# The last column group of x2 turned by VectorE out of DRAM, the loads of two gates moved, one store moved

## The chip, the cores and the metric

The kernel runs on one core of a Trainium2 chip. The metric is device time in microseconds; the median of three runs before the change is 1065.82 us (1065.55 to 1066.18). Times inside the kernel are from one execution taken by the hardware profiler, counted from its first instruction. Engines are called by their names: PE or TensorE (products and transposes), PEld (TensorE's loading of weights), DVE or VectorE, ACT or ScalarE, POOL or GpSimd, SP or SyncE, which only issues DMAs here. ScalarE issues DMAs too; a `q` behind an engine's name in a view (SPq, ACTq) marks what its sequencer issued.

## The reference

One layer of a decoder trunk, 512 tokens (T) by 2048 features (D), in float32:

```
h = rms_norm(x, norm_g);  z = h @ w_in          # RWKV streams, gates, pool input
y_mix = concat([y_rwkv * silu(g_rwkv), y_pool * pool_scale * silu(g_pool)])
x2  = x + y_mix @ w_out
gate = sigmoid(x2 @ w_pg + b_pg)
x3  = x2 + gate * (p @ w_ple)
out = rms_norm(x3, final_g)
```

The change touches only what lies behind the recurrence: x2, the gate, x3 and the last norm.

## The kernel before

**Products in three parts.** Every operand of a large product is split into a high part (a copy rounded to a narrower float32 format) and a low part (the remainder); `mm3` adds high x high, high x low and low x high in PSUM. The copy is ScalarE's, the subtraction VectorE's: `wsplit` (L127 to L136) for a tile of weights, which also issues the load from DRAM on SP's queue, and `split` (L140 to L143) for activations. `wsplit` leaves its three instructions in `wmade`: the DMA, the copy, the subtraction. The pool `wp` has four buffers each for `raw`, `whi` and `wlo`, so copies run up to four steps ahead of TensorE, and loads up to four steps ahead of the copies.

**The two last projections.** `proj` makes one group of 512 output columns: 16 steps over the 128-row slices k of the contraction, in each step four row tiles of 128 tokens (`acc[tt]`), three products each. It runs four times for `w_out` (the products are called `acc_o` in the trace, k in the sequence `order`) and then four times for `w_pg` (`acc_g`, k from 0 to 15). The contraction of `w_pg` runs over the columns of x2, so x2 is needed transposed: `x2hi` and `x2lo`, 16 tiles of 128 columns by 512 tokens. Column group `ec` of `w_out` makes the tiles 4 ec to 4 ec + 3.

**How x2 is transposed.** When a group of `w_out` is done, VectorE adds x (L1123) and ScalarE's queue stores the tile to `x2d` in DRAM (L1124). For the first three groups `turner` does the rest beside the next group's products: at each step `proj` calls `side(i)`, which from step `RD0` = 5 on issues three reads a step on SP's queue (L1135), 16 in all, of 64 KB each. A read brings a 32-row strip of a tile in such a way that VectorE's transpose of 32x32 blocks (L1141, at the steps `TURNS` = 8, 9, 11, 12) then gives the transposed tile, which `split` takes apart. Blocks lie in `x2g`, turned tiles in `x2t`. The last group (ec = 3) has no next group of `w_out`; there `turn` (L1146 to L1152) transposes with TensorE against the identity, 16 times 128x128 into PSUM (`px`), inside the first group of `w_pg`: `proj` calls `aside` at step 2.

**The gates.** For each group and row tile of `w_pg`, `gate` adds `bB` (the bias, VectorE, L1195), takes the tanh (ScalarE, L1197), combines with `pler` (p @ w_ple, made before and kept in DRAM; L1203) and with `x2r` (x2, read back; L1204), squares, and multiplies by `gB`. Their loads are DMAs of ScalarE: `recall` (four `pler`, L1112), `vectors` (`bB` and `gB`, L1171 and L1173), `fetch` (one `x2r` per row tile, L1251).

**What sets the order.** A scheduler sorts each engine's instructions, by program order and by when its model holds them ready; each engine then runs its list in order. `tc.issue_after(i)` puts the instructions of its block that are on `i`'s engine behind `i` in that list. A DMA has to wait for its turn on the queue of the engine that issues it.

**The end.** After the last product the last row tile is scaled and stored in four pieces of 512 columns in the sequence 0, 1, 3, 2, by SP (L1247). Pieces 1 and 2 are scaled by ScalarE, the others by VectorE.

Of the kernel before, what the change touches and what calls it, by code (L numbers as in the profile page):

```python
# [9 lines left out]
F32 = mybir.dt.float32  # L10
# [5 lines left out]
P = 128  # L16
T = 512
D = 2048
KT = D // P
NT = T // P  # L20
# [14 lines left out]
def trunk_kernel(ctx: ExitStack, tc: tile.TileContext, x, p, norm_g, w_in, mu, w0, w_up, a0, a_up,  # L35
                 k_k, k_a, r_k, ln_w, ln_b, w_pool, pool_scale, w_out, w_ple, w_pg, b_pg, final_g, out):
    nc = tc.nc
    PSUM = bass.MemoryType.PSUM
    x, p, w_in, w_out, w_ple, w_pg = x[0], p[0, 0], w_in[0], w_out[0], w_ple[0], w_pg[0]
    out = out[0]  # L40
# [53 lines left out]
    for h in range(2):  # L94
        rows = slice(64 * h, 64 * h + 64)
# [44 lines left out]
    def split(hi, lo, src):  # L140
        c_ = nc.scalar.copy(hi, src)
        nc.vector.tensor_tensor(lo, src, hi.bitcast(F32), ALU.subtract)
        return c_  # L143
# [920 lines left out]
    def proj(w, hi_, lo_, ec, nm, ks=range(KT), tts=range(NT), keep=None, side=None, aside=None):  # L1064
        acc = {tt: acc_tile(f"acc_{nm}{ec}_{tt}") for tt in tts}
        for i, k in enumerate(ks):
            src = w[k * P:(k + 1) * P, ec * EC:(ec + 1) * EC].unsqueeze(1)
            if nm == "o" and ec == 0 and i + AHEAD < KT:
                load_y(ks[i + AHEAD])
            if (f"{nm}{ec}_{k}", 0) in ready:  # L1070
                wh, wl = ready.pop((f"{nm}{ec}_{k}", 0))
            elif nm == "o" and ec == 0 and i < 4:
                wh, wl = chunk(f"{nm}{ec}_{k}", 0)
            elif keep is None or LATE <= i < KT - KEEP:
                wh, wl = wsplit(src, 1, EC, f"{nm}{ec}_{k}")
            else:
                raw = wp.tile([P, 1, EC], F32, name=f"raw_{nm}{ec}_{k}", tag="raw")
                nc.sync.dma_start(out=raw, in_=src)
                if i < 2:
                    if i == 0:  # L1080
                        two = [pp.tile([P, 2, EC], F32R, name=f"{g}k", tag=g, bufs=1) for g in ("dh", "dl")]
                    wh, wl = (g[:, i:i + 1, :] for g in two)
                else:
                    own = i < KT - 4
                    wh, wl = ((kp_ if own else wp).tile([P, 1, EC], F32R, name=f"{g}k{k}",
                                                        tag=f"{g}k{k}" if own else g) for g in ("whi", "wlo"))
                split(wh, wl, raw)
                keep[k] = (wh, wl)
                if i >= LATE:
                    continue  # L1090
            if aside is not None and i == 2:
                with tc.issue_after(e_.ins):
                    hi = aside()
                with tc.issue_after(hi.ins):
                    recall(0, lp)
            if side is not None:
                side(i)
            for tt in tts if keep is None or i >= LATE else tts[:-1]:
                ts_ = slice(tt * P, (tt + 1) * P)
                first = i == (LATE if keep is not None and tt == NT - 1 else 0)  # L1100
                e_ = mm3(acc[tt], hi_[:, k, ts_], lo_[:, k, ts_], wh[:, 0, :], wl[:, 0, :], first, i == KT - 1)
        return acc
# [5 lines left out]
    def recall(ec, pool):  # L1108
        ples[ec] = []
        for tt in range(NT):  # L1110
            t_ = pool.tile([P, EC], F32, name=f"pler{ec}_{tt}", tag="ple", bufs=4)
            nc.scalar.dma_start(out=t_, in_=pled[tt * P:(tt + 1) * P, ec * EC:(ec + 1) * EC])  # L1112
            ples[ec].append(t_)

    for ec in range(D // EC):
        es = slice(ec * EC, (ec + 1) * EC)
        acc = proj(w_out, yhi, ylo, ec, "o", order, side=side)
        x2 = []
        for tt in range(NT):
            rows = slice(tt * P, (tt + 1) * P)  # L1120
            t_ = pp.tile([P, EC], F32, name=f"x2_{ec}_{tt}", tag=("u", "sw")[tt // 2])
            nc.scalar.dma_start(out=t_, in_=x[rows, es])
            nc.vector.tensor_tensor(t_, acc[tt], t_, ALU.add)  # L1123
            nc.scalar.dma_start(out=x2d[ec, :, rows, :].rearrange("c t e -> t c e"),  # L1124
                                in_=t_.rearrange("p (c e) -> p c e", e=P))
            x2.append(t_)

        def turner(blocks, turned, ec=ec):
            parts = [(c, q) for c in range(EC // P) for q in range(4)]

            def side(i):
                with tc.issue_after(wmade[0].ins), tc.issue_after(wmade[1].ins), tc.issue_after(wmade[2].ins):
                    if i >= RD0:
                        for c, q in parts[:RDN]:
                            nc.sync.dma_start(out=blocks[32 * q:32 * q + 32, c],  # L1135
                                              in_=x2d[ec, c].rearrange("(b k) (q i) -> q k b i", k=32, i=32)[q])
                        del parts[:RDN]
                    if i in TURNS:
                        c = TURNS.index(i)
                        t_ = turned(c)  # L1140
                        nc.vector.transpose(t_.rearrange("p (b k) -> p b k", k=32), blocks[:, c])  # L1141
                        split(x2hi[:, 4 * ec + c, :], x2lo[:, 4 * ec + c, :], t_)

            return side

        def turn(ec=ec, x2=x2):  # L1146
            for i in range(EC // P):
                pt = psM.tile([P, T], F32, name=f"px2_{ec}_{i}", tag="m")
                for tt in range(NT):
                    nc.tensor.transpose(pt[:, tt * P:(tt + 1) * P], x2[tt][:, i * P:(i + 1) * P], ident)  # L1150
                hi = split(x2hi[:, 4 * ec + i, :], x2lo[:, 4 * ec + i, :], pt)
            return hi  # L1152

        if ec < D // EC - 1:
            side = turner(ymp.tile([P, EC // P, T // 32, 32], F32, name=f"x2g{ec}", tag="x2g"),
                          lambda i: ymp.tile([P, T], F32, name="x2t", tag="x2t"))
# [4 lines left out]
    with tc.tile_pool(name="fp", bufs=2) as fp, tc.tile_pool(name="kp_", bufs=1) as kp_:  # L1161
        x3 = [fp.tile([P, D], F32, name=f"x3_{tt}", bufs=1) for tt in range(NT)]
        ssq = [fp.tile([P, D // EC + 1], F32, name=f"ssq{tt}", bufs=1) for tt in range(NT)]
        LAST = D // EC - 1
        WIDE, ENDS = 256, 6
        kept = {}

        def vectors(ec):
            es = slice(ec * EC, (ec + 1) * EC)
            bB = fp.tile([P, EC], F32, name=f"bB{ec}", tag="bB")  # L1170
            nc.scalar.dma_start(out=bB, in_=b_pg[0:1, es].to_broadcast([P, EC]))  # L1171
            gB = fp.tile([P, EC], F32, name=f"gB{ec}", tag="gB")
            nc.scalar.dma_start(out=gB, in_=final_g[es].unsqueeze(0).to_broadcast([P, EC]))  # L1173
            return bB, gB

        sq = [None]

        def behind(i, of):

# [52 lines left out]
        def scaled(tt, rs, gts, pcs):  # L1232
            rows = slice(tt * P, (tt + 1) * P)
            for pc_ in pcs:
                ps_ = slice(pc_ * EC, (pc_ + 1) * EC)
                if pc_ == LAST:
                    o_ = 0
                    for g_ in gts:
                        w_ = g_.shape[-1]
                        nc.vector.scalar_tensor_tensor(x3[tt][:, ps_.start + o_:ps_.start + o_ + w_], g_, rs,  # L1240
                                                       vec[1][:, o_:o_ + w_], ALU.mult, ALU.mult)
                        o_ += w_
                elif pc_ in ((1, 2) if tt == NT - 1 else (1,)):
                    nc.scalar.activation(x3[tt][:, ps_], x3[tt][:, ps_], AF.Copy, scale=rs)
                else:
                    nc.vector.tensor_scalar(x3[tt][:, ps_], x3[tt][:, ps_], rs, None, ALU.mult)
                nc.sync.dma_start(out=out[rows, ps_], in_=x3[tt][:, ps_])  # L1247

        def fetch(ec, tt):
            x2_ = fp.tile([P, EC], F32, name=f"x2r{ec}_{tt}", tag="x2r", bufs=4)  # L1250
            nc.scalar.dma_start(out=x2_.rearrange("p (c e) -> p c e", e=P),  # L1251
                                in_=x2d[ec, :, tt * P:(tt + 1) * P, :].rearrange("c t e -> t c e"))
            pre[tt] = (x2_, ple[tt])

        for ec in range(LAST):
            pre = {}
            vec = vectors(ec)
            acc = proj(w_pg, x2hi, x2lo, ec, "g", aside=turn if ec == 0 else None)
            ple = ples.pop(ec)
            recall(ec + 1, fp if ec % 2 == 0 else lp)  # L1260
            for tt in range(NT):
                fetch(ec, tt)
                gate(acc[tt], ec, tt, slice(ec * EC, (ec + 1) * EC), ec)
        ec = LAST
        ple = ples.pop(ec)
# [64 lines left out]
```

## Time and profile before

| what | us |
|---|---|
| median of three runs | 1065.82 (1065.55 to 1066.18) |
| the profiled execution | 1066.03 |
| its span, first to last instruction | 1064.3 |
| products of `w_out` start | 704.4 |
| products of `w_pg` start | 878.4 |
| last product starts | 1055.1 |

The span is that of the instructions; 1.7 us of the execution's own time lie around it. In the views a row of the timeline is: start, length, engine, line, operation, output<-inputs, shape, count, and in brackets the idle time of that engine before it with what ended it. A row "x12" stands for twelve instructions merged. The chain of waits is followed back from the last instruction, at each step to what released it; its pieces are start, length, engine and tile. Lengths of single products overlap, since TensorE takes the next one in before the last has left; the distance of their starts is the pace.

### The profile page before, as it was taken

To read this page: it belongs to the slowest core of one execution; us is meant where nothing else is said; L and a number is where in the kernel's file an instruction comes from. 1 tells how busy PE (TensorE), PEld (TensorE's weight loads), DVE (VectorE), ACT (ScalarE), POOL (GpSimd) and SP (SyncE) were. 2 spreads that over 40 slices of the span, in tenths; PEclk is the share of its full clock that TensorE was granted. 3 is DMA by queue.
4 is the path that set the end of the run, shared out by engine and by line. 5 is a ranking of instruction groups with operands and counts; after the bars stand their busy time and mean duration, and the time that the engine had idled before them with its cause. 6 is when DMAs were issued, how large, how long until landed. Compare 5 with 4: busy or idle time off the path is not lost.

```text
span 1064.3 us, 17220 instructions
## 1 busy us (share of the span) xinstructions
PE 1040.8 (98%) x5884; PEld 861.4 (81%) x5884; DVE 714.1 (67%) x1878; ACT 434.0 (41%) x893; POOL 75.6 (7%) x180
## 2 busy tenths in 40 slices
PE   5999999999999999999999999999999999999996
PEld 4888888888888888878888788888888888888885
DVE  6687878878788689797877968553444343535456
ACT  7633424434334344344442344543222232324336
POOL 2100011010110101201101102000000000000000
PEclk9999999999999999999999999999999999999998
DMA  7444453554555635545447364774846649355434
GB/s 239 108 119 122 124 127 78 156 147 105 163 121 137 157 87 151 144 114 150 117 114 186 84 160 132 240 244 142 208 149 176 173 137 277 125 182 173 155 99 158
DMA packets 292173, 159.08 MB, mean 149 GB/s; under 512 B 130305, under 2 KB 254826, under 8 KB 292086
## 3 DMA queue, kind: packets, MB, share of 16 engines
q1 hardware_dynamic: 264070, 129.41, 44.6%
q10 hardware_dynamic: 28016, 28.58, 8.7%
q8 instruction: 46, 0.75, 0.3%
q14 instruction: 41, 0.34, 0.1%
HBM read 130.63 MB, written 26.79 MB: 148 GB/s over the span
## 4 chain that ended last, share of the span: by engine, by line
PE 84%; DVE 3%; issue 1%; ACT 0%; DMA 0%; ACTq 0%; DVEq 0%
PE acc_o L161 16%; PE acc_g L161 16%; PE zb L161 14%; PE zg L161 7%; PE zv L161 6%; PE zr L161 6%; PE zk L161 6%; PE pple L161 2%; PE py L161 2%; PE pu L161 2%; PE pm L161 1%; PE ps L161 1%; PE pp L161 1%; PE pmv L161 1%; DVE sw L418 1%
## 5 line engine op out<-in xcount | busy, mean ns | idle before, releaser
L134 DVE TENSOR_TENSOR wlo_g<-raw_g,whi_g 128x512 fp32r<-128x512 f32 x84 | 57.3, 689 | 81.5 <-ACT whi_g L133 81.5
L161 PE MATMUL zb<-hhi,whi_b 128*128 128x512 f32 x256 | 105.2, 411 | 0.0
L161 PE MATMUL zb<-hhi,wlo_b 128*128 128x512 f32 x256 | 100.4, 392 | 0.0
L161 PE MATMUL zb<-hlo,whi_b 128*128 128x512 f32 x256 | 99.9, 390 | 0.0
L161 PE MATMUL acc_o<-whi_o,ylo 128*128 128x512 f32 x256 | 99.7, 390 | 0.0
L161 PE MATMUL acc_o<-wlo_o,yhi 128*128 128x512 f32 x256 | 99.7, 389 | 0.0
L134 DVE TENSOR_TENSOR wlo_o<-raw_o,whi_o 128x512 fp32r<-128x512 f32 x64 | 43.9, 690 | 79.3 <-ACT whi_o L133 79.2
L161 PE MATMUL acc_o<-whi_o,yhi 128*128 128x512 f32 x256 | 94.8, 389 | 0.0
L133 ACT CAST whi_g<-raw_g 128x512 fp32r<-128x512 f32 x84 | 51.9, 620 | 103.7 <-PE acc_g L161 57.4
L161 PE MATMUL acc_g<-whi_g,x2hi 128*128 128x512 f32 x208 | 81.3, 391 | 0.0
L161 PE MATMUL acc_g<-wlo_g,x2hi 128*128 128x512 f32 x208 | 81.1, 390 | 0.0
L161 PE MATMUL acc_g<-whi_g,x2lo 128*128 128x512 f32 x208 | 80.8, 390 | 0.0
L904 POOL TENSOR_SCALAR s0p<-sbd,pw 64x64 f32<-64x64 f32 x96 | 57.6, 600 | 324.4 <-DVE sbd L897 246.3
L133 ACT CAST whi_o<-raw_o 128x512 fp32r<-128x512 f32 x64 | 39.4, 621 | 94.2 <-PE acc_o L161 58.4
L133 ACT CAST whi_b<-raw_b 128x512 fp32r<-128x512 f32 x64 | 39.4, 620 | 51.7 <-PE zv L161 16.4
L134 DVE TENSOR_TENSOR wlo_b<-raw_b,whi_b 128x512 fp32r<-128x512 f32 x64 | 43.9, 688 | 21.8 <-ACT whi_b L133 20.8
L721 DVE TENSOR_TENSOR xw<-xw,tm 128x60 f32<-128x60 f32 (+24 forms) x248 | 52.3, 211 | 6.8
L161 PEld LDWEIGHTS zb<-hhi,wlo_b 128*128 128x128 f32 x256 | 48.0, 188 | 10.8
L878 ACT COPY uv<-pu 64x64 f32<-64x64 f32 x128 | 26.3, 205 | 73.4 <-PE pu L161 72.4
L161 PEld LDWEIGHTS acc_o<-whi_o,yhi 128*128 128x128 f32 x256 | 48.1, 188 | 10.0
L161 PEld LDWEIGHTS acc_o<-wlo_o,yhi 128*128 128x128 f32 x256 | 48.1, 188 | 10.0
L161 PEld LDWEIGHTS acc_o<-whi_o,ylo 128*128 128x128 f32 x256 | 48.1, 188 | 9.9
(293 smaller groups left out, 2516.9 us busy)
## 6 DMA issues: line engine op xcount, KB each, us to landing
raw_b<-in_w_in_dram SPq DMA_DIRECT2D x64, 256.0 KB
raw_o<-in_w_out_dram SPq DMA_DIRECT2D x64, 256.0 KB
raw_g<-in_w_pg_dram SPq DMA_DIRECT2D x64, 256.0 KB
raw_k<-in_w_in_dram SPq DMA_DIRECT2D x32, 256.0 KB
raw_r<-in_w_in_dram SPq DMA_DIRECT2D x32, 256.0 KB
raw_v<-in_w_in_dram SPq DMA_DIRECT2D x32, 256.0 KB
raw_g<-in_w_in_dram SPq DMA_DIRECT2D x32, 256.0 KB
bkd<-bk SPq DMA_DIRECT2D x8, 512.0 KB
```

The lines of the kernel that those rows point to most:

```text
L133: made.append(nc.scalar.copy(hi, raw))
L134: made.append(nc.vector.tensor_tensor(lo, raw, hi.bitcast(F32), ALU.subtract))
L161: i = nc.tensor.matmul(*a, **k)
L418: nc.vector.tensor_tensor(n_[:, w_:T], s_[:, w_:T], s_[:, 0:T - w_], ALU.add)
L721: nc.vector.tensor_tensor(xw[:, 0:n_, s + 1:32], xw[:, 0:n_, s + 1:32], tm[:, 0:n_, 0:w_], ALU.add)
L878: u_ = nc.scalar.copy(uv[pb:pb + 64, ch, hc], psu[hc, hc])
L904: nc.gpsimd.tensor_scalar(s0p[hc, :], nxt[hc, hc], pcn[hc], None, ALU.mult)
```

## The change

1. `turn` and its 16 transposes are removed. The last group gets a `turner` of its own, with `x3[0]` for the blocks and slices of `x3[1]` for the turned tiles (both are written only later, by the gates). `proj` of the first group of `w_pg` calls its `side`: reads from step 6 on, three a step, turns at the steps 9, 10, 11 and 13.
2. The first group's `recall` and `vectors`, which stood ahead of the group or at its third step, are issued at its step 12 behind ScalarE's copy of that step's weights (`begin`). The second group's `recall` and the `fetch` of each gate are put behind that copy too.
3. The last row tile's store of piece 2 is issued by ScalarE, not SP.

```diff
-            if aside is not None and i == 2:
-                with tc.issue_after(e_.ins):
-                    hi = aside()
-                with tc.issue_after(hi.ins):
-                    recall(0, lp)
+            if aside is not None and i == 12:
+                with tc.issue_after(wmade[1].ins):
+                    aside(wmade[1])
...
-        def turner(blocks, turned, ec=ec):
+        def turner(blocks, turned, ec=ec, rd0=RD0, rdn=RDN, turns=TURNS):
...
-        def turn(ec=ec, x2=x2):
-            for i in range(EC // P):
-                pt = psM.tile([P, T], F32, name=f"px2_{ec}_{i}", tag="m")
-                for tt in range(NT):
-                    nc.tensor.transpose(pt[:, tt * P:(tt + 1) * P], x2[tt][:, i * P:(i + 1) * P], ident)
-                hi = split(x2hi[:, 4 * ec + i, :], x2lo[:, 4 * ec + i, :], pt)
-            return hi
...
+        side = turner(x3[0].rearrange("p (c b k) -> p c b k", c=EC // P, k=32), lambda i: x3[1][:, i * T:(i + 1) * T],
+                      rd0=6, rdn=3, turns=(9, 10, 11, 13))
...
+        def begin(e_):
+            nonlocal vec
+            recall(0, lp)
+            vec = vectors(0)
+            begun_.append(e_)
...
-                nc.sync.dma_start(out=out[rows, ps_], in_=x3[tt][:, ps_])
+                (nc.scalar if tt == NT - 1 and pc_ == 2 else nc.sync).dma_start(out=out[rows, ps_], in_=x3[tt][:, ps_])
...
-            vec = vectors(ec)
-            acc = proj(w_pg, x2hi, x2lo, ec, "g", aside=turn if ec == 0 else None)
+            if ec:
+                vec = vectors(ec)
+            acc = proj(w_pg, x2hi, x2lo, ec, "g", side=side if ec == 0 else None, aside=begin if ec == 0 else None)
             ple = ples.pop(ec)
-            recall(ec + 1, fp if ec % 2 == 0 else lp)
+            with tc.issue_after(begun_[0].ins):
+                recall(ec + 1, fp if ec % 2 == 0 else lp)
             for tt in range(NT):
-                fetch(ec, tt)
+                with tc.issue_after(begun_[0].ins):
+                    fetch(ec, tt)
                 gate(acc[tt], ec, tt, slice(ec * EC, (ec + 1) * EC), ec)
```

More of the change, by code (lines that the diff above doesn't have):

```diff
@@ L1132, in side @@
                 with tc.issue_after(wmade[0].ins), tc.issue_after(wmade[1].ins), tc.issue_after(wmade[2].ins):
-                    if i >= RD0:
-                        for c, q in parts[:RDN]:
+                    if i >= rd0:
+                        for c, q in parts[:rdn]:
                             nc.sync.dma_start(out=blocks[32 * q:32 * q + 32, c],
                                               in_=x2d[ec, c].rearrange("(b k) (q i) -> q k b i", k=32, i=32)[q])
-                        del parts[:RDN]
-                    if i in TURNS:
-                        c = TURNS.index(i)
+                        del parts[:rdn]
+                    if i in turns:
+                        c = turns.index(i)
                         t_ = turned(c)
@@ L1176, in trunk_kernel @@
         sq = [None]
+        begun_ = []
+        def begin(e_):
[3 more added lines that the diff above has]
+            begun_.append(e_)
+        vec = None
         def behind(i, of):
```

## The prediction

> **What bounds the kernel now.** I read the page's busy shares and chain first, then the chain of waits over the place of the change, then who waits there, then the timeline of each queue that the change touches.
>
> ```profile
> PE 1040.8 (98%) x5884; PEld 861.4 (81%) x5884; DVE 714.1 (67%) x1878; ACT 434.0 (41%) x893; POOL 75.6 (7%) x180
> 704.52 174.08 PE acc_o L161 x768
> 878.60 5.44 PE acc_g L161 x24
> 884.04 1.31 PE px L1150 x12
> 885.35 1.16 PE acc_g L161 x5
> 886.51 0.44 PE px L1150 x4
> 886.95 73.11 PE acc_g L161 x322
> ```
>
> The first row is the page's, the others are pieces of the chain (start, length, what). TensorE is busy 98% of the span, and from 704.5 us the chain is TensorE alone: all of `w_out`, then `w_pg`. 768 products took 174.08 us, so a product starts every 0.2267 us and a step of `proj` (four row tiles, three products each) takes 2.72 us. The only pieces that are not products of the projections are the 16 transposes `px`. What matters here is therefore (a) what TensorE no longer does and (b) whether something new makes it wait.
>
> ```profile
> PEld acc_g L161 <- DVE gt L1195: 0.2, 1, 0.2
> 883.65 0.39 PE L161 MATMUL acc_g<-whi_g,x2lo 128*128 128x512 f32 x1
> 883.88 1.47 PE L1150 MATMUL px<-ident,x 128*128 128x128 f32 x12
> 885.11 0.48 PE L161 MATMUL acc_g<-whi_g,x2hi 128*128 128x512 f32 x1
> 885.43 0.39 PE L161 MATMUL acc_g<-wlo_g,x2hi 128*128 128x512 f32 x1
> 886.12 0.39 PE L161 MATMUL acc_g<-wlo_g,x2hi 128*128 128x512 f32 x1
> 886.35 0.60 PE L1150 MATMUL px<-ident,x 128*128 128x128 f32 x4
> 886.71 0.48 PE L161 MATMUL acc_g<-whi_g,x2lo 128*128 128x512 f32 x1
> 887.02 0.39 PE L161 MATMUL acc_g<-whi_g,x2hi 128*128 128x512 f32 x1
> ```
>
> The first row is the only wait of TensorE in the view of waits from 835 to 930 us: 0.2 us, at the first gates. The rest is its timeline around the transposes.
>
> **Part 1, the transposes go.** From product to product where 0.227 us is usual: 883.65 to 885.11 is 1.23 too long, 885.11 to 885.43 is 0.09, 886.12 to 886.71 is 0.36, 886.71 to 887.02 is 0.08. Together 1.8 us (the chain's `px` pieces alone give 1.31 + 0.44 = 1.75). No wait hides behind them, so this is all that can go: **-1.8 us**.
>
> **Part 2, the blocks from DRAM.** In their place come 16 reads of 64 KB on SP's queue, four transposes on VectorE, and the same four pairs of ScalarE copy and VectorE subtraction, now out of SBUF. The kernel does exactly this already for the first three column groups, beside `w_out`; the last of these stages starts at 704.52 + 3 x 43.52, near 835.0 us.
>
> ```profile
> 838.51 0.33 SPq L130 DMA_DIRECT2D raw_o<-in_w_out_dram  x1
> 840.97 6.75 SPq L1135 DMA_DIRECT2D x2g<-x2d  x9
> 847.82 0.43 SPq L130 DMA_DIRECT2D raw_o<-in_w_out_dram  x1
> 851.78 0.62 ACT L133 CAST whi_o<-raw_o 128x512 fp32r<-128x512 f32 x1 [5.17 <-DMA raw_o<-in_w_out_dram]
> 852.44 0.43 SPq L1135 DMA_DIRECT2D x2g<-x2d  x1
> L1141 DVE STREAM_TRANSPOSE x2t<-x2g x12: 702/704/706, 765.4 to 866.3; 128x512 f32<-128x512 f32 x12
> 869.07 0.68 DVE L142 TENSOR_TENSOR x2lo<-x2t,x2hi 128x512 fp32r<-128x512 f32 x1
> 887.02:924.91 37.89, 37.89 (x169) 31.36 (x168) 12.11 (x19) 10.33 (x17) 0.00 (x0) 1.00 0.64 208
> ```
>
> Here nine reads stood ahead of the weights of step 8 (of 0 to 15), whose copy began at 851.78; with copy and subtraction (0.62 + 0.69) they were there near 853.1. Step 8 runs at 835.0 + 8 x 2.72 = 856.7, so 3.6 us were left, and the chain row of 174.08 us shows that TensorE never waited. In the new stage reads begin one step later, so six instead of nine stand ahead of that load: about 2 us more slack. VectorE gains 4 x 0.70 = 2.8 us, in a stage where it is busy 12.11 of 37.89 us (last row, a window: PE, weight loads, then VectorE).
>
> When must the columns be there? Tile 12 + c of x2 is first used at step 12 + c, and TensorE consumes in order. The last column was done at 869.75, 34.8 us after its stage began, with its turn at step 12; at step 13 that is 37.5 us, and step 15 begins at 40.8 us. Margin 3.3 us for the last column; the first has its turn at step 9 and over 9 us. Cost **0**; below nothing it can't go, and above it goes only if the margin is lost (rivals).
>
> [...]
>
> **Part 3, the loads of the first two gates.** 14 loads wait in ScalarE's order for the 13th copy: four `pler`, `bB`, `gB`, then four `pler` of the next group and four `x2r`.
>
> ```profile
> 880.59 1.04 ACTq L1171 DMA_DIRECT2D bB<-in_b_pg_dram  x1
> 882.49 0.62 ACT L133 CAST whi_g<-raw_g 128x512 fp32r<-128x512 f32 x1 [5.91 <-issue]
> 882.60 0.35 ACTq L1112 DMA_DIRECT2D pler<-pled  x1
> 894.41 2.56 ACTq L1251 DMA_DIRECT2D x2r<-x2d  x3
> 904.93 0.62 ACT L133 CAST whi_g<-raw_g 128x512 fp32r<-128x512 f32 x1 [2.10 <-PE acc_g L161]
> 907.65 0.62 ACT L133 CAST whi_g<-raw_g 128x512 fp32r<-128x512 f32 x1 [2.10 <-PE acc_g L161]
> 922.52 1.28 DVE L1195 TENSOR_TENSOR gt<-acc_g,bB 128x512 f32<-128x512 f32 x2
> 925.11 1.29 DVE L1204 SCALAR_TENSOR_TENSOR gt<-gt,x2r 128x512 f32<-128x512 f32 x2
> 890.70 1.26 ACT L133 CAST whi_g<-raw_g 128x512 fp32r<-128x512 f32 x2 [3.12 <-DMA raw_g<-in_w_pg_dram]
> 905.00:908.00 3.00, 3.00 (x15) 2.49 (x14) 0.69 (x1) 0.90 (x2) 0.00 (x0) 1.00 0.52 184
> 914.00:917.00 3.00, 3.00 (x15) 2.47 (x14) 0.98 (x2) 0.62 (x1) 0.00 (x0) 1.00 0.29 89
> ```
>
> The last two rows are windows of 3 us: busy time of PE, its weight loads, VectorE, ScalarE and GpSimd, the granted clock, the share of the DMA engines, GB/s. Taking them from the start frees ScalarE there (idle 5.91 us in issues before the copy at 882.49), which gives nothing, since TensorE waits for no copy. Nearest to it is the copy of step 6 at 890.70, late for its weights; copied and subtracted by 892.1, it is wanted at 878.44 + 6 x 2.72 = 894.8 once the transposes are gone. Its rivals for the DMA engines, the loads, move away, and the block reads begin behind it. The 13th copy, 904.93 now, falls at 903.1. Behind it ScalarE has 14 issues; from 882.60 to 896.97 it issued 12 of these, 1.2 us each with all that stood between, and 0.35 us is the short end. So 5 to 17 us of issuing in slots that leave 2.1 us between copies. What waits behind: the copies of steps 13 to 15 and the last x2 column. Copy 13 is due at 905.8 and its weights are used at 878.44 + 13 x 2.72 = 913.8, so after 1.3 us of copy and subtraction it may be 6.7 us late. The first six loads at 1.2 us end at 910.9, weights at 912.3: still in time. And the gates: their sum needs `bB` at 922.52 - 1.8 = 920.7, the third operation `x2r` at 923.3. The eleventh load (`x2r` of the first tile) is issued by 903.7 + 11 x 1.2 = 916.9, some 6 us before. Between 905 and 917 the DMA engines now stand at 0.5 falling to 0.3 busy, so I lean to the short end. Cost **0**, with 0 to 8 us as ends.
>
> **Part 4, the last store.**
>
> ```profile
> 1058.20 1.33 ACT L1244 ACTIVATE x<-x,frs 128x512 f32<-128x512 f32 x2 [0.23 <-DVE frs L1229]
> 1058.72 1.80 SPq L1247 DMA_DIRECT2D out_dram<-x  x4
> 1059.50:1062.30 2.80, 0.00 (x0) 0.00 (x0) 0.00 (x0) 0.04 (x1) 0.00 (x0) 0.50 1.00 369
> SPq L1326 <- DMA out_dram<-x: 2.6, 1, 2.6
> ```
>
> SP issues four stores from 1058.72 to 1060.52, 0.45 each; the last one's data are ready at 1059.53, and ScalarE can issue it then, half a microsecond sooner. But the row of the window shows all 16 engines full (share 1.00, 369 GB/s) from 1059.5 to 1062.3, and 4 x 256 KB at that rate are 2.8 us: the stores already queue behind each other. The end hangs on the first store and on the bytes. Ends: 0 and -0.45; I take **-0.1**, near the row.
>
> **Sum.** -1.8 + 0 + 0 - 0.1 = -1.9 us. The profiled execution took 1066.03 us (span 1064.3 and 1.7 around it), which gives 1064.1; the median of the runs is 0.2 lower, 1065.82, and gives **1063.9 us**. A measurement of this kernel tells 0.2% (2.1 us) from no change, so this gain lies just inside "same".
>
> **Rivals.**
> 1. *The last store gains its whole half microsecond* (0.2). For it: it leaves a serial queue. Against it: the full engines. Then 1065.82 - 1.8 - 0.45, about 1063.5: faster.
> 2. *ScalarE issues before it copies* (0.10), the slower side. If the order on ScalarE puts most of the 14 loads ahead of copy 13, TensorE starves at step 13. Seven at 1.2 us end at 912.1 and cost nothing (weights at 913.5); each one more costs 1.2 us; all 14 end at 920.5, weights at 921.9 against 913.8, **8.1 us**, so 1072.0. It is slower than before from the ninth load on (2.1 us), and measurably from the eleventh. Against it: in the old stage copies went between the loads.
> 3. *The gates get `x2r` late* (0.07). VectorE runs in order, so a late `x2r` holds the sums of the other tiles, and TensorE needs the banks: it already waits 0.2 us there. Two microseconds late is 1065.9: no change.
> [...]
> That nothing of the change takes effect is excluded: the transposes are in the chain by name.
>
> **Chances.** My forecast 0.58, the rivals 0.2, 0.10, 0.07 and 0.05. A quarter of the forecast's own spread (0.3 us to either side) lies beyond 0.2%: faster 0.3, same 0.6, slower 0.1. Range 1063.3 to 1065.8: forecast, rival 1 and most of rival 3; of rivals 2 and 4 only what is mild.
>
> **What would show it.** Part 1: no `px` in the chain, one piece of `acc_g` from 878.6 on, and the gates' first sum 1.8 us earlier, at 920.7. Part 2: turns of `x2` on VectorE before step 12, and no wait of TensorE for `x2hi` or `x2lo`. Part 3: copies of steps 13 to 15 between the loads. Part 4: the window of full DMA engines as long as now. I am wrong if TensorE waits anywhere between 878 and 930 us, or if the stretch behind the last product (1055.3 to the end) is shorter by more than 0.2 us.

## The result and the profile after

The changed kernel took 1071.43 us (median of six runs, 1070.66 to 1072.58) against 1065.80 for the kernel before beside it: ratio 1.0052, interval [1.0041, 1.0062]. It is slower by half a per cent, 7.5 us above the forecast and outside the range. The profiled execution took 1071.71 us with a span of 1070.0.

First the chain of waits of the changed kernel from 870 to 960 us, its longest pieces from 878 us on (start, length, what), then who waited for whom on TensorE there.

```profile
878.31 41.49 PE acc_g L161 x183
919.83 0.70 DVE gt L1196
921.22 0.70 DVE gt L1204
923.16 0.68 DVE x L1212
926.38 0.68 DVE gt L1204
927.72 32.41 PE acc_g L161 x133
```

```profile
PE acc_g L161 <- ACT whi_g L133: 4.5, 1, 4.5
PE acc_g L161 <- DVE wlo_g L134: 0.2, 1, 0.2
```

The `px` pieces are gone, and the first group of `w_pg` is one unbroken piece: the 1.8 us were saved. Then the chain leaves TensorE for the first time since 704 us. It goes through the gates of the first group on VectorE and ScalarE, and comes back at 927.7 us. TensorE stood for 4.5 us, waiting for ScalarE's copy of a weight tile.

TensorE's timeline there, and windows of both kernels at that place (PE, PEld, VectorE, ScalarE, GpSimd busy, granted clock, share of the DMA engines, GB/s; the changed kernel first, then the one before):

```profile
921.44 0.39 PE L161 MATMUL acc_g<-whi_g,x2lo 128*128 128x512 f32 x1
926.28 1.22 PE L161 MATMUL acc_g<-whi_g,x2hi 128*128 128x512 f32 x2 [4.45 <-ACT whi_g L133]
927.72 0.80 PE L161 MATMUL acc_g<-wlo_g,x2hi 128*128 128x512 f32 x1 [0.22 <-DVE wlo_g L134]
928.32 0.63 PE L161 MATMUL acc_g<-whi_g,x2lo 128*128 128x512 f32 x1
928.74 0.63 PE L161 MATMUL acc_g<-wlo_g,x2hi 128*128 128x512 f32 x1
...
932.06 0.39 PE L161 MATMUL acc_g<-whi_g,x2hi 128*128 128x512 f32 x1
```

```profile
921.60:926.20 4.60, 0.23 (x2) 0.00 (x0) 4.43 (x8) 2.71 (x8) 0.00 (x0) 0.88 0.53 176
926.20:931.80 5.60, 5.30 (x12) 3.71 (x13) 5.60 (x10) 3.55 (x9) 0.00 (x0) 0.50 0.44 129
```

```profile
921.60:926.20 4.60, 4.60 (x22) 3.82 (x21) 4.19 (x7) 2.39 (x5) 0.00 (x0) 1.00 0.33 110
926.20:931.80 5.60, 5.60 (x27) 4.46 (x26) 5.60 (x11) 3.86 (x10) 0.00 (x0) 1.00 0.54 165
```

From 921.44 to 926.28 no product starts: 4.84 us where 0.23 is usual, so 4.6 lost. Behind it the granted clock is 0.50 and products start every 0.43 us until 932.06, which costs 3.1 more (from 926.28 to 932.06 twelve starts, 5.78 us, at the usual pace 2.72). Twelve starts at 0.43 would be 5.1 us; the other 0.6 or so lie at the first three products, where the low part of the weights is waited for as well (0.22). Lost 7.7, saved 1.8: 5.9, and the spans differ by 5.7.

Why was the weight tile not copied? ScalarE's timeline of the changed kernel:

```profile
911.03 0.62 ACT L133 CAST whi_g<-raw_g 128x512 fp32r<-128x512 f32 x1 [2.09 <-DMA raw_g<-in_w_pg_dram]
...
911.73 1.40 ACTq L1110 DMA_DIRECT2D pler<-pled  x3
913.17 3.35 ACTq L1252 DMA_DIRECT2D x2r<-x2d  x3
920.55 0.63 ACT L1198 ACTIVATE gt<-gt 128x512 f32<-128x512 f32 x1 [8.22 <-DVE gt L1196]
...
925.11 0.61 ACT L1198 ACTIVATE gt<-gt 128x512 f32<-128x512 f32 x1
925.63 1.12 ACT L133 CAST whi_g<-raw_g 128x512 fp32r<-128x512 f32 x2
```

The copy at 911.03 is the first group's last. By the pace of the copies the buffer of the second group's first one came free one step later, near 913.8. In the kernel before, three copies of the second group (915.81 and the two below) came ahead of the first tanh:

```profile
918.53 0.62 ACT L133 CAST whi_g<-raw_g 128x512 fp32r<-128x512 f32 x1 [2.10 <-PE acc_g L161]
921.25 0.62 ACT L133 CAST whi_g<-raw_g 128x512 fp32r<-128x512 f32 x1 [2.10 <-PE acc_g L161]
923.24 1.23 ACT L1197 ACTIVATE gt<-gt 128x512 f32<-128x512 f32 x2 [1.36 <-DVE gt L1195]
```

Here the scheduler put the tanh of the first gates (L1198) ahead of them. The tanh waits for the gate's sum, the sum for the end of the first row tile's products at 919.8, and ScalarE, which runs its list in order, issued its last load ahead of the tanh until 916.5 and then stood idle to 920.55, with the copies waiting behind it. Three tanh and two squares later, at 925.63, the copy came.

### The profile page after: what moved, and what is told of

Read it like the earlier page. It is cut to its first block, busy times and chain, and to the rows that moved or that the text cites. A ratio compares the mean times of both kernels' runs of the same rounds, so it can differ in the third digit from the quotient of the medians.

```text
span 1070.0 us, 17226 instructions
## 1 busy us (share of the span) xinstructions
PE 1042.2 (97%) x5868; PEld 861.2 (80%) x5868; DVE 717.0 (67%) x1882; ACT 434.4 (41%) x893; POOL 75.6 (7%) x180
## 4 chain that ended last, share of the span: by engine, by line
PE 83%; DVE 3%; issue 1%; ACT 0%; DMA 0%; DVEq 0%; SPq 0%
PE acc_o L161 16%; PE acc_g L161 16%; PE zb L161 14%; PE zg L161 7%; PE zv L161 6%; PE zr L161 6%; PE zk L161 6%; PE pple L161 2%; PE py L161 2%; PE pu L161 2%; PE pm L161 1%; PE ps L161 1%; PE pp L161 1%; PE pmv L161 1%; PE pq L161 0%
```

## The experiments

Theory A: that order on ScalarE is the loss. Rival B: the loads themselves come too late. Rival C: the turning of x2 and its reads hold something up. Ratios are to the kernel before, run beside each.

**1. The order held.** The changed kernel, with the tanh behind the second group's third copy. The dependency added is one of the list's order alone (`NoSync`); `ths` holds the tanh instructions:

```diff
             elif keep is None or LATE <= i < KT - KEEP:
                 wh, wl = wsplit(src, 1, EC, f"{nm}{ec}_{k}")
+                if nm == "g" and ec == 1 and i == 2:
+                    for tt in tts:
+                        tc.add_manual_dep(ths[0, tt].ins, wmade[1].ins.name, mybir.DependencyInfo(
+                            mybir.DependencyClass.NoSync, mybir.DependencyReason.DATA))
...
             th = nc.scalar.activation(gt, gt, AF.Tanh, scale=0.5)
+            ths[ec, tt] = th
```

> The changed kernel whole, with its 14 loads where they are, and one thing added: the tanh of the first group's gates stands behind the copy of the second group's third weight tile in ScalarE's list. Theory A (the second group's copies stood in ScalarE's list behind the gates' tanh, and so waited for the end of the first group): the stretch without products at 921.4 us is gone, the transposes stay saved, about 1064.0 us. Rival B (the loads themselves come too late, for the gates or for the weights): nothing is moved, about 1071.4. Rival C (the turning of x2 on VectorE and its reads hold something up): about 1071.4.

Measured: 1064.37 us, ratio 0.9983 [0.9973, 0.9992]. Its chain over the place, then ScalarE's rows:

```profile
878.12 87.04 PE acc_g L161 x384
```

```profile
913.00 3.03 ACTq L1258 DMA_DIRECT2D x2r<-x2d  x4
919.54 1.67 ACT L133 CAST whi_g<-raw_g 128x512 fp32r<-128x512 f32 x3 [7.40 <-DMA x2r<-x2d]
921.12 1.15 ACT L1203 ACTIVATE gt<-gt 128x512 f32<-128x512 f32 x2
```

TensorE runs from 878 us through both groups without a wait, with the same 14 loads at the same place and the same turning. A holds; B and C fall as causes of the stop. The copies come only at 919.54, since the last loads still hold ScalarE, some 2 us before the group that needs them (878.12 + 43.52 = 921.64): the cover is thin.

**2. The order alone, on the kernel before.** The copies of steps 0 to 3 of the second group go behind the third and the fourth tanh, where the changed kernel has them (`ths` as above):

```diff
-                wh, wl = wsplit(src, 1, EC, f"{nm}{ec}_{k}")
+                with tc.issue_after(ths[0, 2 + i // 2].ins) if nm == "g" and ec == 1 and i < 4 else ExitStack():
+                    wh, wl = wsplit(src, 1, EC, f"{nm}{ec}_{k}")
```

> The kernel before the change, with one thing added: the copies of the second group's first four weight tiles stand in ScalarE's list behind the tanh of the third and fourth gate, as the changed kernel has them. A: TensorE stops at the end of the first group for some 5 us and is slow for some more, 1065.8 + 7.5, about 1073. B and C: no load and no turn is touched, 1065.8.

Measured: 1076.87 us, ratio 1.0096 [1.0079, 1.0112]. Its windows and waits:

```profile
923.60:929.50 5.90, 0.40 (x2) 0.00 (x0) 5.80 (x10) 3.47 (x9) 0.00 (x0) 0.78 0.56 176
929.50:937.20 7.70, 6.45 (x14) 4.62 (x15) 5.08 (x9) 2.83 (x8) 0.00 (x0) 0.50 0.60 169
```

```profile
PE acc_g L161 <- ACT whi_g L133: 5.6, 1, 5.6
PE acc_g L161 <- DVE wlo_g L134: 1.2, 1, 1.2
```

The order by itself makes the stop and the half clock in a kernel with nothing else changed. It costs 10 us rather than the 7.5 expected: the first wait is a microsecond longer than in the changed kernel, and so is the second, for a low part.

**3. The loads put back.** The changed kernel, with `vectors` ahead of each group, `recall(0)` at step 2, and nothing held:

```diff
-            if aside is not None and i == 12:
+            if aside is not None and i == 2:
...
             recall(0, lp)
-            vec = vectors(0)
...
-            if ec:
-                vec = vectors(ec)
+            vec = vectors(ec)
...
-            with tc.issue_after(begun_[0].ins):
-                recall(ec + 1, fp if ec % 2 == 0 else lp)
+            recall(ec + 1, fp if ec % 2 == 0 else lp)
             for tt in range(NT):
-                with tc.issue_after(begun_[0].ins):
-                    fetch(ec, tt)
+                fetch(ec, tt)
```

> The changed kernel with the 14 loads issued near the group's start again, as before the change; x2 still turned by VectorE, last store on ScalarE. A and B: about 1064.0 us. C: about 1071.4, since the turning is still there.

Measured: 1070.47 us, ratio 1.0038 [1.0023, 1.0053]. The 1064.0 that A and B gave is missed. It is nearly C's number, but not C's mechanism: here another wait stops TensorE. SP's rows, ScalarE's copies of steps 7 and 8, and three windows:

```profile
884.20 1.86 SPq L1133 DMA_DIRECT2D x<-x2d  x3
888.38 0.35 SPq L130 DMA_DIRECT2D raw_g<-in_w_pg_dram  x1
892.10 1.60 SPq L1133 DMA_DIRECT2D x<-x2d  x3
896.38 0.35 SPq L130 DMA_DIRECT2D raw_g<-in_w_pg_dram  x1
```

```profile
894.19 0.62 ACT L133 CAST whi_g<-raw_g 128x512 fp32r<-128x512 f32 x1 [6.30 <-DMA raw_g<-in_w_pg_dram]
903.19 0.62 ACT L133 CAST whi_g<-raw_g 128x512 fp32r<-128x512 f32 x1 [8.38 <-DMA gB<-in_final_g_dram]
```

```profile
890.00:894.00 4.00, 4.00 (x20) 3.30 (x19) 0.00 (x0) 0.00 (x0) 0.00 (x0) 1.00 1.11 269
898.00:902.00 4.00, 2.20 (x10) 1.50 (x8) 0.00 (x0) 0.00 (x0) 0.00 (x0) 1.00 1.14 298
902.00:906.00 4.00, 2.14 (x4) 1.45 (x5) 0.69 (x1) 0.62 (x1) 0.00 (x0) 0.56 1.20 193
```

With the 14 loads at the start again the share of the DMA engines is above 1 from 886 to 910 us (1.04 to 1.23 in windows of 4 us; in the changed kernel only from 890 to 894, 1.18). SP's list stretches (six reads and two weight loads take 12.5 us, where the changed kernel issues all 16 reads with their four weight loads in the 12.2 us from 883.47 to 895.65), and the weights of step 8 are copied at 903.19. TensorE's last product before them starts at 899.81, the next at 903.86. The clock falls to half again (a mean of 0.51 from 903.8 to 909.4). So the turning and the move of the loads belong together: each loses without the other or without the right order.

**4. The loads alone moved,** on the kernel before, with the transposes on TensorE (the hunks of the change for `begin`, `recall` and `fetch`).

> The kernel before the change with the 14 loads moved behind the copy of step 12 and nothing else; the transposes stay on TensorE. In this kernel's list the second group's first three copies stand ahead of the gates' tanh, as before the change. A: 1065.8 us, the late loads cost nothing by themselves. B: as late as in the changed kernel, 1071.4 + 1.8, about 1073. C: 1065.8.

Measured: 1067.64 us, ratio 1.0015 [1.0006, 1.0024]. ScalarE's row, VectorE's rows, and TensorE's only wait:

```profile
921.44 1.67 ACT L133 CAST whi_g<-raw_g 128x512 fp32r<-128x512 f32 x3 [6.98 <-DMA x2r<-x2d]
```

```profile
922.09 1.90 DVE L134 TENSOR_TENSOR wlo_g<-raw_g,whi_g 128x512 fp32r<-128x512 f32 x3 [6.91 <-ACT whi_g L133]
923.90 1.28 DVE L1205 TENSOR_TENSOR gt<-acc_g,bB 128x512 f32<-128x512 f32 x2
```

```profile
PE acc_g L161 <- DVE gt L1205: 0.4, 1, 0.4
```

No long stop, so not B's 1073. But not free either, as A had it: three copies queue behind the last loads, VectorE subtracts them in a row, and the gates' sums come at 923.90 instead of 922.52. TensorE then waits 0.4 us for a gate's sum. The kernel is about 1.5 us slower than the one before. Of this the trace shows 0.6 at that wait (product starts at 928.83 and 929.65, where 0.23 is usual); where the rest lies is open.

**5. Position and dose.** The changed kernel with one number changed (`i == 12` to 10, or to 6), and with the loads split (the first group's six at step 2, the other eight at 12):

```diff
-            if aside is not None and i == 12:
+            if aside is not None and i == 2:
                 with tc.issue_after(wmade[1].ins):
                     aside(wmade[1])
+            if aside is not None and i == 12:
+                begun_.append(wmade[1])
...
             vec = vectors(0)
-            begun_.append(e_)
```

> The changed kernel with one number changed: the loads of the first two gates wait for the copy of step 10, not 12, which is behind the last block read either way. In this kernel's list on ScalarE the second group's first three copies come ahead of the gates' tanh without being told to. A (order on ScalarE): no stop of TensorE near 921 us, about 1064.3 us as with the order held. If instead the late position of the loads matters by itself, between 1064.3 and 1071.4.

> The changed kernel with the loads behind the copy of step 6, near 886 us, in the midst of the 16 block reads; the copies stand ahead of the tanh here too. A alone: about 1064.3. D (loads and block reads at one time crowd out the weights on the DMA engines and in SP's list, as when the loads were put back): TensorE stops around step 8 or 9, 1066 to 1071.

> The changed kernel with the 14 loads split: the first group's six (four pler, bB, gB) behind the copy of step 2, near the block reads, the other eight behind the copy of step 12. The second group's copies stand ahead of the gates' tanh in this list. D (loads and block reads at one time crowd out the weights) is a matter of dose: six early loads beside 16 reads, less than half of the early ones put back before, so a stop of TensorE of 0 to 2 us instead of 4: 1064 to 1067. If any early load is enough, 1070 as with all of them early; if D is wrong, 1064.2.

Measured: at 10, 1064.17 us, 0.9984 [0.9974, 0.9993]; at 6, 1071.75 us, 1.0055 [1.0041, 1.0070]; split, 1064.09 us, 0.9979 [0.9969, 0.9989]. The chain at 10 and ScalarE's rows there, the chain of the split kernel, and ScalarE's rows and TensorE's waits of the one at 6:

```profile
878.42 81.60 PE acc_g L161 x360
```

```profile
919.26 0.62 ACT L133 CAST whi_g<-raw_g 128x512 fp32r<-128x512 f32 x1 [1.20 <-PE acc_g L161]
920.66 1.31 ACT L1198 ACTIVATE gt<-gt 128x512 f32<-128x512 f32 x2 [0.78 <-DVE gt L1196]
```

```profile
877.55 82.51 PE acc_g L161 x364
```

```profile
891.42 3.65 ACTq L1110 DMA_DIRECT2D pler<-pled  x4
898.81 0.62 ACT L133 CAST whi_g<-raw_g 128x512 fp32r<-128x512 f32 x1 [6.80 <-DMA pler<-pled]
906.09 0.62 ACT L133 CAST whi_g<-raw_g 128x512 fp32r<-128x512 f32 x1 [6.66 <-DMA raw_g<-in_w_pg_dram]
```

```profile
PE acc_g L161 <- ACT whi_g L133: 4.2, 2, 3.1
```

Two steps earlier, behind the reads, the scheduler puts three copies (the last at 919.26) ahead of the tanh by itself, and the stop is gone. In the midst of the reads the collision of experiment 3 returns (copy of step 9 at 906.09; the last product before it starts at 903.27), a little above the range expected of it. The first group's six loads at the start cost nothing. They were all issued by 882.5, ahead of the first block read at 883.24, whereas in experiment 3 the other eight were issued amid the reads, from 884 to 896. So the collision came with those eight; whether their number or their moment counts these runs don't tell, nor whether the DMA engines' throughput or the turn in SP's list sets it.

**6. The store.** Alone on the kernel before, and the kernel with the order held with the store back on SP:

```diff
-                nc.sync.dma_start(out=out[rows, ps_], in_=x3[tt][:, ps_])
+                (nc.scalar if tt == NT - 1 and pc_ == 2 else nc.sync).dma_start(out=out[rows, ps_], in_=x3[tt][:, ps_])
```

> The kernel before the change with the last row tile's store of piece 2 on ScalarE and nothing else. If the stores are bound by the 16 full DMA engines: within 0.2 us of 1065.8. If SP's serial issue held the end: 0.45 us less. In the changed kernel's profile the stretch behind the first of the last four stores was not shorter, so rather the first.

> The kernel with the order held and the last store on SP again: the turn and the loads alone. The transposes' 1.8 us stay saved: about 1064.3 us, the same as with the store on ScalarE within 0.3.

Measured: alone 1065.80 us, ratio 0.9999 [0.9990, 1.0009]; order held with the store on SP 1064.00 us, 0.9984 [0.9975, 0.9993]. A window of the changed kernel behind its first of the last four stores:

```profile
1065.10:1067.90 2.80, 0.00 (x0) 0.00 (x0) 0.00 (x0) 0.00 (x0) 0.00 (x0) 0.50 1.01 369
```

It is the same 2.8 us at 369 GB/s as before: who issued the store made no difference here.

## Why the prediction was wrong

**Part 1, right.** No `px`, first gates' sum at 919.83 (forecast 920.7; the group starts 0.3 us earlier, and the sum of the kernel before, from which I took it, stood 0.6 us behind a subtraction at 921.91), and with the copies ahead of the tanh TensorE keeps the saving: four kernels came out at 1064.0 to 1064.4 us, 1.9 to 2.2 under the kernel before beside them, where the forecast was 1.9 under.

**Part 2, right in this kernel, but it hangs on the move of the loads, to which I gave no price.** Turns from 895.9 us on, no wait for x2. The 16 reads were issued in 12.2 us, the last column was there at 913.05 and first used near 919.1 (878.31 + 15 x 2.72). Time was lost beside the reads in experiment 3 and at step 6 (TensorE waited 3.7 and 4.2 us), but only with loads issued among them: what it waited for was not the columns but the weights behind the reads. I had written that taking the loads from the start "gives nothing". It gives the 1.8 us their room: with the loads left there the kernel is at 1070.5 us.

**Part 3 is the step that failed.** "What waits behind: the copies of steps 13 to 15 and the last x2 column", cost 0. The list went too short: behind the loads stand the second group's copies as well, and beside them the gates' tanh, whose place in ScalarE's list the scheduler chooses anew. Rival 2 had the right engine, the right kind (work that waits queued ahead of copies) but put it at copy 13 of the first group, where the copies did go between the loads (905.75, 908.32). It got one chance in ten. That its price is so near (8.1 us and 1072.0; measured 7.7 and 1071.4) is luck: its 8.1 us were all waiting, the measured ones 4.6 of a stop and 3.1 behind it. What the profile before showed and I did not use: the second group's copies lay 1.4 us (921.25 + 0.62 to 923.24) ahead of the tanh in a list that the change was to reorder.

The half clock was not in the sum either, nor in the price of rival 2. Rival 3 did not happen in this kernel, where TensorE waited for no gate; in experiment 4 it did, with 0.4 us. Nor were the block reads late in this kernel, which had the chance of 0.05: no product waited for a column of x2.

**Part 4, right.** No gain to be measured from the store, and the window is as long as before, so rival 1 falls.

Why the scheduler takes the tanh first with the loads at 12, and not at 10 or with the transposes on TensorE, is open: its model's times are in no trace.

## What to carry to other kernels

Where a scheduler orders each engine's list, list behind a moved block all that follows on its engine up to the next instruction that waits for another engine, the next group's work too, and price the case that this instruction comes first. Then test the order by a dependency on it before giving up a change: here one edge, or loads issued two steps earlier, turned +0.5% into -0.2%. And when work moves from an engine to the DMA queues, the transfers that share its time are a part of the change, not a separate one.

## What the runs showed of the hardware

In these runs a long stop of TensorE cost more than itself: in the changed kernel 4.6 us of stop and 3.1 behind it. With waits of 3.1, 3.7, 4.5 and 5.6 us (loads at step 6, experiment 3, the changed kernel, experiment 2) the granted clock fell to 0.50, and in the changed kernel products then started every 0.43 us instead of 0.23; with a wait of 0.4 us (experiment 4) it stayed at 1.00. What a wait between 0.4 and 3.1 us does is not shown. Windows of the kernel with the loads at step 6, at the two ends of its half clock:

```profile
906.50:907.00 0.50, 0.24 (x1) 0.21 (x1) 0.26 (x1) 0.21 (x1) 0.00 (x0) 0.88 1.14 193
910.00:911.00 1.00, 1.00 (x5) 0.77 (x5) 0.00 (x0) 0.00 (x0) 0.00 (x0) 0.86 0.87 134
```

A mean of 0.88 in a window that starts at 1.00 and ends at 0.50 puts the change at 906.9, and 0.86 puts the way back at 910.3. Worked out alike, the half clock lasted from 902.5 to 909.3 in experiment 3 (0.56 from 902 to 906, 0.59 from 906 to 910), from 925.1 to 931.9 in the changed kernel (0.61 from 925.0 to 925.5, 0.56 from 931.5 to 932.0), and in experiment 2 from 926.9 (0.78 from 923.6 to 929.5) to 937.1 at least (0.50 from 929.5 to 937.2, where the window ends). That is 3.4, 6.8, 6.8 and at least 10.2 us, the second and third twice the first. The clock fell 3.6, 2.7 and 3.7 us after the start of the last product (loads at step 6, experiment 3, the changed kernel). What sets these times, and why the half clock lasted 3.4 us in one run and at least three times as long in another, is not shown.
